# Keeping the second softmax map's exponentials in PSUM, and a third buffer for turned probabilities

## The chip, the cores and the metric

The kernel runs on one core of one Trainium2 chip. The core has a matrix engine (TensorE, in the profile PE, with PEld for its weight loads), a vector engine (DVE), an activation engine (ACT), a general engine (POOL) and a queue that issues DMA transfers (SP). SBUF is the working memory; PSUM is the memory that matmuls write, of which this kernel uses eight banks. The metric is the time of one execution on the device in microseconds (us); the time given is the median of several runs.

## The reference

Two layers over 512 latent tokens and 256 context tokens of width 1024, all in 32 bits. Layer 0 mixes tokens by differential attention, layer 1 by grouped-query attention with normed queries and keys. The change touches layer 0:

```python
def diff(qq, kk, vv, gate):
    o1 = sweep_attention(qq[..., 0, :], kk[..., 0, :], vv)
    o2 = sweep_attention(qq[..., 1, :], kk[..., 1, :], vv)
    o = o1 - lam.astype(o1.dtype) * o2
    o = rms_norm(o, subln_g) * (1.0 - lam_init)
    o = o.reshape(o.shape[0], o.shape[1], BRANCH_WIDTH)
    return (o * jax.nn.silu(gate)) @ w_out

y = diff(q, k_all, v_all, z)
yc = diff(qc, kc, vc, zc) if with_ctx_out else None
```

Each of the 8 heads has two maps of queries and keys, 64 wide, and one value of width 128. `sweep_attention` is softmax attention. Latent queries read 768 keys (latent and context), context queries read the 256 context keys. Around the mixer stand an adaptive norm before, projections of width 4096 into queries, keys, values and gate, an output projection, a norm after, and the gated residual.

## The kernel before

**The work in layer 0.** A head's attention is cut into units of 128 queries: four units (`s_units`, `unit(qt)`) for the latent queries, of which the last two (`CTX_AT`) carry 128 context queries along in heads 0 to 6. In head 7 the context queries have two small units of their own (`unit_last`). One unit does this, for the two maps m = 0 and 1:

- PE writes the scores of both maps into two PSUM tiles `sc[0]` and `sc[1]` of two banks each (`s_mm`, twelve matmuls, 18 with context queries). There are only these two tiles, so the next unit writes the same ones. The first matmul of a block writes `sc[1]`. Four more banks (`bk`) serve all other matmuls.
- DVE takes the maximum of each row, ACT the exponential with that maximum as bias and the row's sum as second output. For m = 0 it goes to one half of the pair tile `pp`, for m = 1 to a tile `p` (tag `p1`, two buffers). For context queries m = 0 goes to a tile of tag `p0`, m = 1 into the tile `ct` (tag `at128`), which later takes the turned probabilities.
- DVE inverts the sums and, for m = 1, multiplies by minus lambda (`nlam`). POOL scales the first map (`scaled(EP0, ...)`). Then one DVE operation combines them: pp = p * factor + pp. This is called the combination here.
- After two units `turn` transposes the pair tile in blocks on DVE, stores it to DRAM (`dr<-pp`) and loads it back in four transfers (`at<-dr`), so that keys lie on partitions. `at` has `ATB` = 2 buffers of 6144 bytes a partition; the two `p1` buffers have 3072 each.
- `pv_steps` splits `at` into a rounded part `ah` and a rest `al` (ACT and DVE), which PE multiplies with the values, three matmuls for a product.

Every product in the kernel is such a sum of three matmuls of rounded parts. PE also does the projections of queries, keys, values and gate for later heads in the same stretch; their weights come by DMA as `raw` and are split into `whi` and `wlo` by ACT and POOL or DVE. Tiles of tag `tmp`, three buffers, serve the swapped queries, the gate's silu, the squares of the head norm and others.

**What sets the order.** The program lists every operation first (`Plan`), with a duration for each by kind and size and the operations that it must wait for: those whose data it needs and those that still use its buffer. PSUM counts by bank: operations of different engines on one bank follow each other. `flow` lists the steps of the streams (scores, turned tiles, value products, others) by due times, with the projections between them. `plan` then simulates all engines, each taking the ready operation of the smallest key. The keys come from the best of twelve passes; then each number in `MOVES` seeds one random shift of some keys (`shift`), on PE or on DVE, ACT, POOL or SP. The resulting order is fixed in the program for each engine and for SP. The program's waits are made from the same list.

In the profile nearly all instructions have line L519, that of the helper which issues them, so the groups are told apart by tile names.

Of the kernel before, what the change touches and what calls it, by code (L numbers as in the profile page):

```python
# [9 lines left out]
F32 = mybir.dt.float32  # L10
F32R = mybir.dt.float32r
AF = mybir.ActivationFunctionType
# [4 lines left out]
P = 128  # L17
# [3 lines left out]
C = 256  # L21
T = 768
# [63 lines left out]
ATB = 2  # L86
# [8 lines left out]
def f32(ap):  # L95
# [37 lines left out]
SLACK = 0  # L133


# [470 lines left out]
def tile_backbone(  # L606
# [25 lines left out]
    def nm(s):  # L632
        uid[0] += 1
        return f"{s}_{uid[0]}"
# [7 lines left out]
    def small(n=1, tag="sm"):  # L642
        return sm.tile([P, 8], F32, tag=tag, name=nm("sm"), bufs=dict(sm=8, ss=6, l=6, mx=6, nmx=4)[tag])[:, :n]
# [19 lines left out]
    def sc2():  # L663
        scs.append(scs.pop(0))
        return scs[-1]
# [21 lines left out]
                d, b = o, a[:, e * 256:e * 256 + 256]  # L687
            nc.tensor.matmul(d, v[:, kt + e, c], b, start=first and i == 0, stop=last and i == 5)

    def turn(pool, pp, w=384, at=None):  # L690
        flat = pp.rearrange("p b u x -> p (b u x)")
        nc.vector.transpose(flat, flat)
        if at is None:
            at = pool.tile([P, 4, w], F32, tag=f"at{w}", name=nm("at"), bufs=ATB if w == 384 else 1)
        for lo in range(0, 4, 4 // DRSPLIT):
            n = 4 // DRSPLIT
            dr = drp.tile([P // DRSPLIT, 4 * 384], F32, tag="dr", name=nm("dr"), bufs=DRB)[:, :4 * w]
            nc.sync.dma_start(dr, flat[32 * lo:32 * (lo + n), :])
            for a in range(4):
                nc.sync.dma_start(  # L700
                    at[32 * a:32 * a + 32, lo:lo + n, :],
                    dr.rearrange("(q j) (a c) -> a j q c", j=32, c=w)[a])
        return at
# [9 lines left out]
    def unit_view(pp, u):  # L713
        return pp[:, :, u, :]
# [542 lines left out]
    for pr in range(NQT):  # L1257
        kts = (2 * pr, 2 * pr + 1)
        if pr + 1 < NQT:
            cs = nxt  # L1260
# [39 lines left out]
    with pl.pool("t0") as t0:  # L1300
# [147 lines left out]
        def s_mm(sc, h, qt, lo, w, prev):  # L1448
            qh, ql, kh_, kl_ = qk[h]
            tok = slice(qt * P, (qt + 1) * P)  # L1450
            for i, (a, b) in enumerate(((qh, kh_), (qh, kl_), (ql, kh_))):
                for m in (1, 0):
                    r = slice(m * 64, m * 64 + 64)
                    o = flat_sc(sc[m])[:, lo:lo + w]
                    if qt < NQ:
                        b_ = b[r, lo:lo + w]
                    else:
                        o, b_ = by_a(o, 64), by_a(b[r, :], 192)[:, :, P:]
                    with after(prev), chained(prev):
                        prev = nc.tensor.matmul(o, a[r, tok], b_, start=i == 0, stop=i == 2)  # L1460
            return prev

        def flat_sc(t):
            return t.rearrange("p j n -> p (j n)")
# [3 lines left out]
        def s_units(h, qts):  # L1468
            res, pair = [], {}
            if qts[0] == 0:  # L1470
                ctx_at[h] = []

            def unit(qt):
                e = CTX_AT.get(qt) if h < KT - 1 else None
                l = small(4, "l")
                sc = [sc2(), sc2()]
                prev = s_mm(sc, h, qt, 0, 512, None)
                prev = s_mm(sc, h, qt, 512, C, prev)
                if e is not None:
                    s_mm(sc, h, NQ + e, T, C, prev)  # L1480
                if (h, qt) in GRP_AT:
                    grp_mm(GRP_AT[h, qt])
                if e is not None:
                    if e == 0:
                        ctx_tiles[h] = (
                            t0.tile([P, 8, 2, 32], F32, tag="p0", name=nm("pp"), bufs=1),
                            t0.tile([P, 4, P], F32, tag="at128", name=nm("at"), bufs=1))
                    cp_, ct = ctx_tiles[h]
                    cs = [unit_view(cp_, e), ct.rearrange("p a c -> p (a c)")[:, e * C:e * C + C].rearrange("p (b x) -> p b x", x=32)]
                if qt % 2 == 0:  # L1490
                    pair[0] = t0.tile([P, 24, 2, 32], F32, tag="pp", name=nm("pp"), bufs=PPB)
                ps_ = [unit_view(pair[0], qt % 2), t0.tile([P, T], F32, tag="p1", name=nm("p"), bufs=2).rearrange("p (b x) -> p b x", x=32)]
                n = 1 if e is None else 2
                for m in range(2):
                    mx = small(2, "mx")
                    for j in range(n):
                        src = flat_sc(sc[m])[:, j * T:j * C + T]
                        nc.vector.tensor_reduce(mx[:, j:j + 1], src, AX.X, ALU.max, negate=True)
                        nc.scalar.activation(
                            (cs if j else ps_)[m], src.rearrange("p (b x) -> p b x", x=32), AF.Exp, bias=mx[:, j:j + 1],  # L1500
                            accum_out=l[:, 2 * m + j:2 * m + j + 1])
                    r = l[:, 2 * m:2 * m + n]
                    nc.vector.reciprocal(r, r)
                    if m == 1:
                        nc.vector.tensor_scalar(r, r, nlam, None, ALU.mult)
                    for j in range(n):
                        d, a = (cs if j else ps_)[0], (cs if j else ps_)[1]
                        if m == 0:
                            scaled(EP0, d, d, r[:, j:j + 1])
                        else:  # L1510
                            nc.vector.scalar_tensor_tensor(d, a, r[:, j:j + 1], d, ALU.mult, ALU.add)
                if qt % 2:
                    res.append(turn(t0, pair[0]))
                if e == 1:
                    ctx_at[h].append(turn(t0, cp_, P, ct))

            def unit_last(qt):
                if qt == NQ:
                    sts["sc"] = sc2()
                    pair[2] = t0.tile([P, 2, C], F32, tag="p0", name=nm("p"), bufs=1)  # L1520
                l = small(2, "l")
                qh, ql, kh_, kl_ = qk[h]
                tok, prev, ps_ = slice(qt * P, (qt + 1) * P), None, []
                sc = sts["sc"]
                for i, (a, b) in enumerate(((qh, kh_), (qh, kl_), (ql, kh_))):
                    for m in (1, 0):
                        r = slice(m * 64, m * 64 + 64)
                        with after(prev), chained(prev):
                            prev = nc.tensor.matmul(k_a_j(sc[:, m, :C]), a[r, tok], by_k(b[r, :], 2), start=i == 0, stop=i == 2)
                for m in range(2):  # L1530
                    mx = small(1, "mx")
                    nc.vector.tensor_reduce(mx, sc[:, m, :C], AX.X, ALU.max, negate=True)
                    if m == 0:
                        pt = pair[2][:, qt - NQ]
                    else:
                        pt = t0.tile([P, T], F32, tag="p1", name=nm("p"), bufs=2)[:, :C]
                    nc.scalar.activation(pt, sc[:, m, :C], AF.Exp, bias=mx, accum_out=l[:, m:m + 1])
                    ps_.append(pt)
                    r = l[:, m:m + 1]
                    nc.vector.reciprocal(r, r)  # L1540
                    if m == 0:
                        scaled(EP0, pt, pt, r)
                    else:
                        nc.vector.tensor_scalar(r, r, nlam, None, ALU.mult)
                        nc.vector.scalar_tensor_tensor(ps_[0], pt, r, ps_[0], ALU.mult, ALU.add)
                res.append(ps_[0])

            if qts[0] == NQ:
                if h < KT - 1:
                    return ctx_at[h], []  # L1550
                sts = {}
                return res, [Step(lambda qt=qt: unit_last(qt), 0.5) for qt in qts]
            return res, [Step(lambda qt=qt: unit(qt), 1.2 + 0.4 * (h < KT - 1 and qt in CTX_AT) + 1.0 * ((h, qt) in GRP_AT)) for qt in qts]

        def pv_steps(h, at, ch, after, ts, ms):
# [164 lines left out]
        for h in range(KT):  # L1720
            per = ATT + DL0[h] + sum(7.7 if f[0] == 'z' else 15.4 for f in HF0[h] if f != ('qk', 1))
            span = per - GAP0
            for ch in range(3):
                at, u = s_units(h, (2 * ch, 2 * ch + 1))
# [97 lines left out]
    for qi, (c, n) in enumerate(OUTC[:2]):  # L1822
        w = get_wout(0, c, n) if qi else w_o
# [18 lines left out]
    c, n = OUTC[2]  # L1842
    w = get_wout(0, c, n)
# [73 lines left out]
    with pl.pool("t1", "right") as t1p:  # L1917
# [281 lines left out]
        for h in range(KT):  # L2199
            p, j = h // 2, h % 2  # L2200
# [3 lines left out]
            for ch in range(2):  # L2204
                at, u = s1_units(h, (2 * ch, 2 * ch + 1))
# [21 lines left out]
        for qi, (c, n) in enumerate(OUTC1):  # L2227
            w = get_wout(1, c, n) if qi else w_o
# [3 lines left out]
            for m in range(NQ):  # L2232
# [13 lines left out]
                if qi == 2:  # L2246
# [6 lines left out]
                    for j in (1, 0):  # L2253
                        for h in range(2 if m == NQ - 1 else 1):
                            w_ = 256 if m == NQ - 1 else 512
                            a = h * w_
# [124 lines left out]
```

## Time and profile before

| | |
|---|---|
| median of 3 runs | 743.32 us (740.20, 743.32, 744.13) |
| the profiled execution's own time | 740.91 us |
| its span, from the first to the last instruction | 739.1 us |
| granted TensorE clock | 0.998 |
| DMA | 133.85 MB, 181 GB/s in the mean |

The profile shows one execution. "Busy" is the time in which an engine had an instruction running. Matmuls are pipelined and their ends modelled, so that a busy PE need not be at its peak. Rows of the timeline give start, duration, engine, line, operation, tile written <- tiles read, shapes and count, and in brackets the idle time before with what ended it. Rows of waits give who waited for whom: us in total, times, longest.

### The profile page before, as it was taken

To read this page: it belongs to the slowest core of one execution; us is meant where nothing else is said; L and a number is where in the kernel's file an instruction comes from. 1 tells how busy PE (TensorE), PEld (TensorE's weight loads), DVE (VectorE), ACT (ScalarE), POOL (GpSimd) and SP (SyncE) were. 2 spreads that over 40 slices of the span, in tenths; PEclk is the share of its full clock that TensorE was granted. 3 is DMA by queue.
4 is the path that set the end of the run, shared out by engine and by line. 5 is a ranking of instruction groups with operands and counts; after the bars stand their busy time and mean duration, and the time that the engine had idled before them with its cause. 6 is when DMAs were issued, how large, how long until landed. Compare 5 with 4: busy or idle time off the path is not lost. (4 is left out here: it accounts for less than half of the span.)

```text
span 739.1 us, 13953 instructions
## 1 busy us (share of the span) xinstructions
PE 726.0 (98%) x5030; PEld 651.1 (88%) x5030; DVE 551.7 (75%) x882; ACT 478.4 (65%) x1085; POOL 461.8 (62%) x506
## 2 busy tenths in 40 slices
PE   7999999999999999999999999999999999999996
PEld 6789888889888889888988998899999989898986
DVE  5454897969979796688887843689666789988834
ACT  6635557876678564676749853695366678788641
POOL 4454887788598856669753311466889969665201
PEclk9999999999999999999999999999999999999999
DMA  9932446255648387473757162453437678888503
GB/s 352 407 134 100 143 132 212 96 162 184 230 142 250 127 246 216 131 228 136 228 150 229 50 236 86 144 179 115 143 129 231 175 237 244 230 259 255 154 29 114
DMA packets 52884, 133.85 MB, mean 181 GB/s; under 512 B 6608, under 2 KB 28368, under 8 KB 51280
## 3 DMA queue, kind: packets, MB, share of 16 engines
q1 hardware_dynamic: 49248, 127.82, 54.1%
q10 hardware_dynamic: 3568, 5.16, 2.2%
q8 instruction: 39, 0.64, 0.4%
q14 instruction: 29, 0.24, 0.1%
HBM read 98.61 MB, written 30.15 MB: 174 GB/s over the span
## 5 line engine op out<-in xcount | busy, mean ns | idle before, releaser
L519 PE MATMUL bk<-whi,h 128*128 128x256 f32 (+1 forms) x1184 | 244.9, 298 | 2.6 <-ACT h L519 1.3
L519 PE MATMUL bk<-h,whi 128*128 128x512 f32 (+2 forms) x832 | 222.6, 348 | 0.0
L519 POOL TENSOR_TENSOR wlo<-raw,whi 128x256 fp32r<-128x256 f32 x200 | 169.2, 869 | 53.1 <-ACT whi L519 52.2
L519 PEld LDWEIGHTS bk<-whi,h 128*128 128x128 f32 x1184 | 191.0, 189 | 11.9 <-ACT h L519 2.1
L519 PE MATMUL bk<-wlo,h 128*128 128x256 f32 (+1 forms) x592 | 174.7, 298 | 0.0
L519 PEld LDWEIGHTS bk<-h,whi 128*128 128x128 f32 x832 | 144.7, 188 | 14.9 <-issue 1.7
L519 PE MATMUL bk<-h,wlo 128*128 128x512 f32 (+2 forms) x416 | 144.1, 348 | 0.0
L519 DVE TENSOR_REDUCE sm<-sc 128x1 f32<-128x768 f32 (+1 forms) x128 | 101.9, 813 | 21.0 <-PE sc L519 14.1
L519 PEld LDWEIGHTS bk<-wlo,h 128*128 128x128 f32 x592 | 111.1, 188 | 4.0
L519 DVE TENSOR_TENSOR al<-at,ah 128x512 fp32r<-128x512 f32 x103 | 96.2, 952 | 19.2 <-ACT ah L519 11.6
L519 POOL TENSOR_SCALAR pp<-pp,sm 128x768 f32<-128x768 f32 (+1 forms) x78 | 77.5, 996 | 52.6 <-DVE sm L519 29.7
L519 PEld LDWEIGHTS bk<-h,wlo 128*128 128x128 f32 x416 | 78.3, 188 | 7.0
L519 ACT CAST whi<-raw 128x1024 fp32r<-128x1024 f32 (+1 forms) x70 | 71.7, 1025 | 17.5 <-PE bk L519 7.8
L519 ACT CAST ah<-at 128x512 fp32r<-128x512 f32 x103 | 61.6, 621 | 9.8 <-PE bk L519 5.7
L519 DVE STREAM_TRANSPOSE pp<-pp 128x1536 f32<-128x1536 f32 (+1 forms) x39 | 61.4, 1575 | 3.8 <-POOL pp L519 3.7
L519 POOL TENSOR_TENSOR sz<-sz,za 128x384 f32<-128x384 f32 (+1 forms) x24 | 30.4, 1265 | 38.3 <-ACT za L519 31.6
L519 PEld LDWEIGHTS sc<-qk,qk 64*128 64x128 f32 x480 | 37.3, 185 | 15.8 <-ACT p L519 3.2
L519 ACT ACTIVATE jk<-bk 128x128 f32<-128x128 f32 (+4 forms) x66 | 22.7, 345 | 43.9 <-PE bk L519 25.6
L519 PE MATMUL sc<-qk,qk 64*128 64x256 f32 (+1 forms) x480 | 48.4, 338 | 1.1 <-ACT p L519 1.0
L519 ACT ACTIVATE pp<-sc,sm 128x768 f32<-128x768 f32 (+1 forms) x46 | 35.5, 772 | 20.2 <-DVE sm L519 20.1
L519 DVE SCALAR_TENSOR_TENSOR pp<-p,sm,pp 128x768 f32<-128x768 f32 x32 | 43.6, 1363 | 3.2 <-POOL pp L519 2.4
L519 ACT ACTIVATE za<-za 128x384 f32<-128x384 f32 (+1 forms) x72 | 39.8, 560 | 5.2 <-DVE za L519 4.9
(213 smaller groups left out, 1353.2 us busy)
## 6 DMA issues: line engine op xcount, KB each, us to landing
dr<-pp SPq DMA_DIRECT2D x32, 768.0 KB, 4.2
at<-dr SPq DMA_DIRECT2D x128, 192.0 KB, 4.6
raw<-in_a_w SPq DMA_DIRECT2D x30, 512.0 KB, 4.4
araw<-in_ada_g SPq DMA_DIRECT2D x12, 1024.0 KB, 6.2
raw<-in_b_w SPq DMA_DIRECT2D x20, 512.0 KB, 3.7
ag<-in_ada_s SPq DMA_DIRECT2D x16, 512.0 KB, 9.5
raw<-in_w_out SPq DMA_DIRECT2D x16, 512.0 KB, 3.8
sw<-qr ACTq DMA_DIRECT2D x32, 128.0 KB, 3.1
```

What stands on the lines that cost most here:

```text
L519: self.ops.append(getattr(eng, meth)(*args, **kw))
```

## The change

- In `unit`, the second map's exponentials (m = 1) are written over their own scores in `sc[1]`, for latent and for context queries. The combination reads them there: one input from PSUM, one from SBUF. So `sc[1]` is in use until the combination has ended, where it was in use until the exponential had. `ct` is written by its transfers alone.
- The tile of tag `p1` is gone. `unit_last`, which used it too, takes a tile of tag `tmp`.
- `turn` has a parameter for the number of buffers of `at`. Layer 0 passes 3, which takes the bytes that `p1` had; layer 1 keeps 2.
- `MOVES` is longer: its 308 numbers are kept, and 207 are added behind them. No operation is added or taken away, and the list of operations is in the same order; the order within each engine comes out anew from the plan.

```diff
-    855299187, 174445339, 702593093, 709254020, 236711175, 391571874)
+    855299187, 174445339, 702593093, 709254020, 236711175, 391571874, 802471119, 806597346, 795014970, 909414891,
...
+    426925270, 219226640, 492092606)

-    def turn(pool, pp, w=384, at=None):
+    def turn(pool, pp, w=384, at=None, n=ATB):
...
-            at = pool.tile([P, 4, w], F32, tag=f"at{w}", name=nm("at"), bufs=ATB if w == 384 else 1)
+            at = pool.tile([P, 4, w], F32, tag=f"at{w}", name=nm("at"), bufs=n if w == 384 else 1)
...
-                    cs = [unit_view(cp_, e), ct.rearrange("p a c -> p (a c)")[:, e * C:e * C + C].rearrange("p (b x) -> p b x", x=32)]
+                    cs = unit_view(cp_, e)
...
-                ps_ = [unit_view(pair[0], qt % 2), t0.tile([P, T], F32, tag="p1", name=nm("p"), bufs=2).rearrange("p (b x) -> p b x", x=32)]
+                ps_ = unit_view(pair[0], qt % 2)
...
+                        src = src.rearrange("p (b x) -> p b x", x=32)
                         nc.scalar.activation(
-                            (cs if j else ps_)[m], src.rearrange("p (b x) -> p b x", x=32), AF.Exp, bias=mx[:, j:j + 1],
+                            src if m else cs if j else ps_, src, AF.Exp, bias=mx[:, j:j + 1],
                             accum_out=l[:, 2 * m + j:2 * m + j + 1])
...
-                        d, a = (cs if j else ps_)[0], (cs if j else ps_)[1]
+                        d = cs if j else ps_
                         if m == 0:
                             scaled(EP0, d, d, r[:, j:j + 1])
                         else:
+                            a = flat_sc(sc[m])[:, j * T:j * C + T].rearrange("p (b x) -> p b x", x=32)
                             nc.vector.scalar_tensor_tensor(d, a, r[:, j:j + 1], d, ALU.mult, ALU.add)
                 if qt % 2:
-                    res.append(turn(t0, pair[0]))
+                    res.append(turn(t0, pair[0], n=3))
...
-                        pt = t0.tile([P, T], F32, tag="p1", name=nm("p"), bufs=2)[:, :C]
+                        pt = t0.tile([P, 512], F32, tag="tmp", name=nm("p"), bufs=3)[:, :C]
```

20 rows, old and new, of the table MOVES are left out of this document.

## The prediction, made before any run of the changed kernel

> **What bounds the kernel now.** I read the page's busy times first, then busy time by stretch (65 to 408 us holds the first layer's attention, 408 to 700 us its output and most of the second layer), then the waits of the weight loads in the same two stretches.
>
> ```profile
> PE 726.0 (98%) x5030; PEld 651.1 (88%) x5030; DVE 551.7 (75%) x882; ACT 478.4 (65%) x1085; POOL 461.8 (62%) x506
> 65.00:408.00 343.00, 341.88 (x2396) 299.76 (x2396) 282.90 (x419) 227.73 (x491) 248.41 (x229) 1.00 0.57 177
> 408.00:700.00 292.00, 290.38 (x1992) 272.38 (x1991) 221.93 (x361) 204.23 (x503) 178.31 (x217) 1.00 0.58 180
> ```
>
> After each stretch's length come the busy times of PE, PEld, DVE, ACT and POOL. In the stretch that the change touches PE stands still for 343.00 - 341.88 = 1.12 us, in the next for 292.00 - 290.38 = 1.62 us. DVE is busy for 82% of the first stretch, POOL for 72%, and both stay behind PE. So PE's own work bounds the kernel. What an edit off PE can win is the wait in front of PE. Of the waits before weight loads (us, times, longest) these are the two of score blocks for exponentials from 65 to 408 us, and the four longest after 408 us:
>
> ```profile
> PEld sc L519 <- ACT p L519: 3.2, 7, 0.8
> ...
> PEld sc L519 <- ACT at L519: 1.2, 2, 0.8
> ```
>
> ```profile
> PEld bk L519 <- ACT sz L519: 1.2, 2, 1.0
> PEld bk L519 <- ACT ah L519: 0.7, 2, 0.4
> PEld bk L519 <- DVE kn L519: 0.6, 1, 0.6
> PEld sc L519 <- ACT pp L519: 0.6, 2, 0.4
> ```
>
> Nine score blocks of layer 0 wait for the exponentials of the unit before: 3.2 + 1.2 = 4.4 us. The four rows of the rest come to 3.1 us. That is 7.5 us in all, my upper end for what better orders can take away, since a weight load partly waits under a matmul that still runs; the smaller measure is PE's own idle time, 1.12 + 1.62 = 2.74 us.
>
> **The change part by part.** One unit (one head, 128 queries) of layer 0, PE, DVE, ACT and POOL rows together, starts at 221.55 us:
>
> ```profile
> 221.55 1.32 PE L519 MATMUL sc<-qk,qk 64*128 64x512 f32 x12
> ...
> 223.27 1.80 DVE L519 TENSOR_REDUCE sm<-sc 128x1 f32<-128x768 f32 x2
> ...
> 224.24 0.90 ACT L519 ACTIVATE pp<-sc,sm 128x768 f32<-128x768 f32 x1
> ...
> 225.13 0.89 ACT L519 ACTIVATE p<-sc,sm 128x768 f32<-128x768 f32 x1
> ...
> 225.41 0.63 PE L519 MATMUL bk<-h,whi 128*128 128x512 f32 x2
> ...
> 225.64 0.19 PEld L519 LDWEIGHTS bk<-h,wlo 128*128 128x128 f32 x1
> 225.71 1.07 POOL L519 TENSOR_SCALAR pp<-pp,sm 128x768 f32<-128x768 f32 x1 [0.62 <-DVE sm L519]
> 225.87 0.39 PE L519 MATMUL bk<-h,wlo 128*128 128x512 f32 x1
> ...
> 226.42 1.31 PE L519 MATMUL sc<-qk,qk 64*128 64x512 f32 x12
> ...
> 226.81 1.02 DVE L519 SCALAR_TENSOR_TENSOR pp<-p,sm,pp 128x768 f32<-128x768 f32 x1 [0.25 <-POOL pp L519]
> ```
>
> The two bk rows of PE in between show its pace: two 512-wide matmuls begin within 225.87 - 225.41 = 0.46 us. Now the second map's exponentials go to SBUF (p), so the next unit's scores start at 226.42, 0.40 us after the exponential ends (225.13 + 0.89 = 226.02) and before the combining operation on DVE (pp from p, sm, pp) has begun.
>
> *The new wait.* With p in the scores' place, the next scores must wait for that operation: here until 226.81 + 1.02 = 227.83, 6.28 us after the unit's start where it was 4.87. This is the shortest chain a unit can have as the engines stand: two maxima, two exponentials, POOL's scaling of the first map, the combination. Behind a waiting score matmul stands every later one of PE's program, and whatever waits for their results; so the chain costs nothing only if other matmuls are put in front. Is there room? The last head is the tightest place (PE's four blocks and a later row, the DVE rows, POOL's, POOL's scaling as a group with busy us and mean ns after its first bar, and the score matmuls in the tile's view: min/median/max, first and last start):
>
> ```profile
> 368.48 1.32 PE L519 MATMUL sc<-qk,qk 64*128 64x512 f32 x12
> ...
> 373.11 1.31 PE L519 MATMUL sc<-qk,qk 64*128 64x512 f32 x12
> ...
> 379.24 1.33 PE L519 MATMUL sc<-qk,qk 64*128 64x512 f32 x12 [0.61 <-ACT p L519]
> ...
> 383.91 1.31 PE L519 MATMUL sc<-qk,qk 64*128 64x512 f32 x12
> ...
> 411.76 0.51 PE L519 MATMUL bk<-h,whi 128*128 128x384 f32 x2
> ```
>
> ```profile
> 373.72 2.68 DVE L519 SCALAR_TENSOR_TENSOR pp<-p,sm,pp 128x768 f32<-128x768 f32 x1
> ...
> 379.88 1.01 DVE L519 SCALAR_TENSOR_TENSOR pp<-p,sm,pp 128x768 f32<-128x768 f32 x1
> ...
> 386.34 1.01 DVE L519 SCALAR_TENSOR_TENSOR pp<-p,sm,pp 128x768 f32<-128x768 f32 x1
> ```
>
> ```profile
> 373.76 1.84 POOL L519 TENSOR_TENSOR gT<-gT,sz 128x768 f32<-128x768 f32 x1
> 378.60 0.91 POOL L519 TENSOR_SCALAR pp<-pp,sm 128x768 f32<-128x768 f32 x1 [3.00 <-DVE sm L519]
> ```
>
> ```profile
> L519 POOL TENSOR_SCALAR pp<-pp,sm 128x768 f32<-128x768 f32 x64 | 67.5, 1055 | 52.6 <-DVE sm L519 29.7 <-PE bk L519 5.4 <-ACT sz L519 3.6
> ```
>
> ```profile
> L519 PE MATMUL sc<-qk,qk x480: 270/280/502, 72.7 to 393.9; 64*128 64x256 f32 x96, 64*128 64x512 f32 x64
> ```
>
> The blocks stand 4.63, 6.13 and 4.67 us apart; at 6.4 us each (6.28 and a hand-over) the three move by 1.8, 0.3 and 1.7, 3.8 us together. Projection matmuls of the gate (bk from h, whi, 384 wide) still run at 411.76, 27 us after the last block, and need no score; they can go in front. Over all heads there is more room: from the first of the 480 score matmuls, 72.7, to head 7's at 368.48 are seven heads, 42.3 us each, and their four units take about 30: two of 6.4, and two with context queries of about 8.5, an estimate (four operations 256 wide more, some half a microsecond each). So I put the wait's exposed part at what the nine waiting blocks gain in scatter: POOL's scaling takes 1055 ns in the mean against 0.91 us at 378.60, 0.145 us more. 9 x 0.145 = 1.3 us. Ends: 0 (all covered) and 3.8 + 1.3 = 5.1 us (head 7 uncovered). Late next would be POOL's scaling, which now stands in PE's way and used to be free to wait.
>
> *The prices of the operations.* From the groups (busy us and mean ns after the first bar), and from the tile's view:
>
> ```profile
> L519 DVE TENSOR_REDUCE sm<-sc 128x1 f32<-128x768 f32 x96 | 88.8, 945 | 13.8 <-PE sc L519 13.2
> ...
> L519 DVE SCALAR_TENSOR_TENSOR pp<-p,sm,pp 128x768 f32<-128x768 f32 x32 | 43.6, 1363 | 3.2 <-POOL pp L519 2.4
> ...
> L519 ACT ACTIVATE p<-sc,sm 128x768 f32<-128x768 f32 x32 | 28.8, 900 | 2.8 <-DVE sm L519 2.8
> ...
> L519 DVE SCALAR_TENSOR_TENSOR pp<-at,sm,pp 128x256 f32<-128x256 f32 x14 | 9.7, 691 | 0.0
> ...
> L519 DVE TENSOR_TENSOR u<-bk,gate 128x512 f32<-128x512 f32 x10 | 6.9, 686 | 17.3 <-ACT jk L519 17.3
> ```
>
> ```profile
> L519 DVE SCALAR_TENSOR_TENSOR pp<-p,sm,pp x32: 1006/1077/2682, 78.1 to 391.9; 128x768 f32<-128x768 f32 x32
> ```
>
> The combination with both inputs in SBUF takes 1.01 us alone and 2.68 beside POOL's 1.84 us multiply. With one input in PSUM the nearest rows are u from bk and gate (512 wide, 686 ns) and the maximum from sc (768 wide, 945 ns); on their line 768 wide costs about 0.95 us and 256 wide 0.43. DVE is relieved of 32 x (1.36 - 0.95) + 14 x (0.69 - 0.43) = 13.1 + 3.6 = 17 us. None of it is on PE's path, so I count 0; ends 0 and what it lets the orders win, counted there. [...]
>
> The exponential into PSUM has no row: ACT never writes PSUM here. I take the 0.90 us of its SBUF form, the nearest; the upper end is 1.80, if one bank served its read and its write in turns; a little less than 0.90 is not excluded and would win nothing on PE. At 0.90 the sum is 0. [...]
>
> *The third buffer* (at, turned probabilities). Who waits for the present two? Of the tile's readers and of the DMA queue, 65 to 408 us:
>
> ```profile
>   DMA at<-dr: 1.4, 1
> ```
>
> ```profile
> SPq L519 <- DMA dr<-pp: 41.0, 14, 6.2
> ...
> SPq L519 <- DVE al L519: 0.9, 1, 0.9
> ```
>
> A reader waited for the transfer once, 1.4 us, and PE not at all. The loads of at wait for their own store (dr from pp, 41 us). Only one wait ended with the last reader, al: 0.9 us. So 0 for the time; the ends are -0.9 and 0. An earlier load issues no more DMAs, but their order with the weight loads on SP can change.
>
> *The last head's context units* put p (256 wide, two of them) among the three "tmp" buffers: 0, since gate work covers it; if that were gone, one combination, 0.5 us.
>
> *The orders.* Some 207 further shifts change priorities on all queues, in both layers. No row prices them. I take the smaller measure of PE's idle time away, -2.7 us, because only that is PE time; ends -7.5 and +2.7 (as much idle time again, since the old shifts were drawn for another graph of waits).
>
> Sum: +1.3 + 0 + 0 + 0 + 0 - 2.7 = -1.4 us. The profiled execution took 740.91 us (span 739.1), so 739.5; the median of the three runs, 743.32, lies 2.4 us above it, so I predict 743.3 - 1.4 = 741.9 us. Runs 740.2 to 744.1 us apart let no difference under about 0.5%, 3.7 us, be told from none.
>
> **The rivals.** *Slower: scores wait for the combination.* Place: the blocks of the last head and others as close. Price: 3.8 + 1.3 = 5.1 us with nothing won back, 748.4 us. For it: the present distances of 4.63 and 4.67 us are shorter than the chain. Against it: 27 us of gate work to put between. It decides once PE stands more than 3.7 us longer before scores.
>
> *Faster: all the waits go.* DVE's 17 us and the spare buffer let the orders take the 7.5 us of weight-load waits, at the chain's cost of 1.3: 743.3 - 6.2 = 737.1 us. For it: PEld is busy for only 299.76 of 343 us. Against: a 512-wide matmul holds PE for 0.23 us and its weight load takes 0.19, so weight loading idles where PE does not; PE is idle for 1.12 us. [...]
>
> *The exponential in place is slow* (1.80 us). Then the chain is 7.3 us, the three blocks of head 7 move by 2.7 + 1.2 + 2.6 = 6.5, and the time is 743.3 + 6.5 + 1.3 = 751.1 us. Nothing in the rows speaks for it but that none speaks against.
>
> **How the numbers follow.** Forecast (within 3.7 us of before) 0.53, faster rival 0.28, wait rival 0.15, slow exponential 0.04. So faster by over 0.5% 0.28, within 0.53, slower 0.19. The range takes in the faster rival, with the ends of third buffer and orders down to 743.3 - 7.5 - 0.9 = 734.9, and the wait rival up to 748.4. The forecast's own range is 739.6 to 747.0.
>
> **What would show it.** Combinations of about 0.95 us, none near 2.7; exponentials onto sc at 0.90; weight loads before scores that wait for DVE pp where they waited for ACT p, near 5.7 us in sum; score blocks in the last head 6.4 us apart or more; PE still idle for about 1 us in layer 0. I am wrong if PE's idle time in layer 0 grows by more than 3.7 us, or if the span shrinks where PE was already full.

## The result, and the profile after

Six runs of the changed kernel took 747.85 to 754.07 us, median 751.03; six of the kernel before on the same chip 740.20 to 744.13, median 742.27. The ratio is 1.0114, with a 95% interval of 1.0078 to 1.0149: slower by 1.1%, where no change within 0.5% (741.9 us) was predicted. On another chip (below) it was 746.90 to 740.60, ratio 1.0077 (1.0053 to 1.0101). The profiled execution took 751.58 us, its span is 749.8 where it was 739.1.

The page's busy times of the changed kernel, and then busy time by stretch (after each stretch's length PE, PEld, DVE, ACT, POOL, then granted clock, DMA share, GB/s):

```profile
PE 731.7 (98%) x5030; PEld 651.9 (87%) x5030; DVE 543.9 (73%) x882; ACT 479.8 (64%) x1085; POOL 446.7 (60%) x506
```

By stretch:

```profile
65.00:408.00 343.00, 336.40 (x2362) 294.31 (x2361) 258.83 (x393) 219.22 (x468) 225.86 (x227) 1.00 0.55 172
408.00:700.00 292.00, 291.29 (x1986) 270.84 (x1985) 224.61 (x371) 209.03 (x515) 183.92 (x220) 1.00 0.58 178
```

PE has the same 5030 matmuls and now stands still for 343.00 - 336.40 = 6.60 us in layer 0, where it was 1.12; in the next stretch for 0.71 where it was 1.62. So the idle time that came is made before 408 us. It is half of the profile's loss: of the 10.7 us by which the span grew, 5.0 are idle time of PE and 5.7 are PE's own busy time (726.0 to 731.7). The granted clock was 0.995 where it was 0.998, worth about 2 us by my estimate (749.8 x 0.005 - 739.1 x 0.002); the rest of the busy time was not traced.

DVE's relief came and bought nothing. Its combinations fell from 43.6 + 9.7 to 32.4 + 6.6 us, 14.3 us less, and its busy time over the whole execution by 7.8 us, since other operations of it took longer. (The 24 us by which the first stretch fell, 282.90 to 258.83, also hold work that moved out of the stretch.)

Who made PE wait from 65 to 408 us (us, times, longest), first in the kernel before, then in the changed one:

```profile
PE sc L519 <- ACT p L519: 1.0, 2, 0.6
```

```profile
PE bk L540 <- ACT sz L540: 3.8, 3, 3.2
PE sc L540 <- DVE pp L540: 2.0, 3, 0.9
PE bk L540 <- ACT arow L540: 0.5, 1, 0.5
PE bk L540 <- DVE al L540: 0.2, 1, 0.2
```

And the weight loads of score blocks, for the combination, where the prediction looked for 5.7 us:

```profile
PEld sc L540 <- DVE pp L540: 3.7, 6, 1.2
```

The second row of PE's is the wait that the change adds. The first holds one wait of 3.22 us, which can be followed back through three engines. Rows of the timeline of DVE, POOL, ACT and PE, in that order:

```profile
220.39 5.27 DVE L540 TENSOR_TENSOR al<-at,ah 128x512 fp32r<-128x512 f32 x1
225.58 2.36 DVE L540 STREAM_TRANSPOSE pp<-pp 128x1536 f32<-128x1536 f32 x2
...
228.76 0.54 DVE L540 SCALAR_TENSOR_TENSOR za<-sz,za 128x384 f32<-128x384 f32 x1
...
220.45 1.87 POOL L540 TENSOR_TENSOR qk<-qr,qk 128x768 fp32r<-128x768 f32 x1
222.26 2.85 POOL L540 TENSOR_TENSOR wlo<-raw,whi 128x256 fp32r<-128x256 f32 x4
...
229.34 0.52 ACT L540 ACTIVATE za<-za 128x384 f32<-128x384 f32 x1 [5.35 <-DVE za L540]
...
232.51 0.50 PE L540 MATMUL bk<-h,whi 128*128 128x256 f32 x2 [3.22 <-ACT sz L540]
```

A subtraction that takes 692 ns in the median lasts 5.27 us. It ends 0.55 us after the last of five POOL instructions that run back to back beside it. I call that a hold: an operation that lasts far longer than its like while another engine works. DVE's next operations come late, ACT stands before `za` and with it its copy `sz` of a PSUM bank, which frees the bank that PE needs.

The operations' prices (min/median/max in ns) are as forecast, combination and exponential in place:

```profile
L540 DVE SCALAR_TENSOR_TENSOR pp<-sc,sm,pp x46: 443/1007/1020, 72.4 to 405.5; 128x768 f32<-128x768 f32 x32, 128x256 f32<-128x256 f32 x14
...
L540 ACT ACTIVATE sc<-sc,sm x46: 434/865/888, 70.4 to 402.4; 128x768 f32<-128x768 f32 x32, 128x256 f32<-128x256 f32 x14
```

### The profile page after: what moved, and what is told of

It reads as the page before. It is cut to its first block, busy times and chain, and to the rows that moved or that the text cites. A ratio compares the mean times of both kernels' runs of the same rounds, so it can differ in the third digit from the quotient of the medians.

```text
span 749.8 us, 13948 instructions
## 1 busy us (share of the span) xinstructions
PE 731.7 (98%) x5030; PEld 651.9 (87%) x5030; DVE 543.9 (73%) x882; ACT 479.8 (64%) x1085; POOL 446.7 (60%) x506
## 4 chain that ended last, share of the span: by engine, by line
PE 48%; ACT 1%; DVE 1%; issue 1%; DMA 1%; DVEq 0%; ACTq 0%
PE bk L540 39%; PE sc L540 9%; DMA araw<-in_ada_g 1%; DVE pp L540 0%; DVE sm L540 0%; DVE al L540 0%; ACT jk L540 0%; ACT pp L540 0%; ACT za L540 0%; DVE u L540 0%; ACT sm L540 0%; ACT ah L540 0%; ACT whi L540 0%; ACT qk L540 0%; ACT sz L540 0%
## 5 line engine op out<-in xcount | busy, mean ns | idle before, releaser
L540 PE MATMUL bk<-h,whi 128*128 128x512 f32 (+2 forms) x832 | 226.1, 350 | 4.0 <-ACT sz L540 3.4
L540 POOL TENSOR_TENSOR wlo<-raw,whi 128x256 fp32r<-128x256 f32 x200 | 164.6, 848 | 41.6 <-ACT whi L540 36.0
L540 POOL TENSOR_SCALAR pp<-pp,sm 128x768 f32<-128x768 f32 (+1 forms) x78 | 74.9, 965 | 60.9 <-DVE sm L540 58.8
L540 DVE TENSOR_TENSOR al<-at,ah 128x512 fp32r<-128x512 f32 x103 | 97.7, 967 | 13.2 <-ACT ah L540 10.7
L540 POOL TENSOR_TENSOR sz<-sz,za 128x384 f32<-128x384 f32 (+1 forms) x24 | 28.1, 1171 | 44.0 <-ACT za L540 42.5
L540 DVE SCALAR_TENSOR_TENSOR pp<-sc,sm,pp 128x768 f32<-128x768 f32 (+1 forms) x46 | 38.2, 847 | 4.5 <-POOL pp L540 2.8
```

Source lines behind the costliest of these rows:

```text
L540: self.ops.append(getattr(eng, meth)(*args, **kw))
```

## The experiments

Theory O: the loss lies in the new orders. Theory W: it lies in the scores' longer hold, whatever the order. Theories C, N and S came up on the way. Every kernel ran in five rounds beside the kernel before, on several chips; ratios are to the kernel before on the same chip. The code shown is shortened: where an edit changes an operation, the order is still planned with the operation as it was, and only what is issued in that order changes.

### The orders as they stand: the long hold and the start

The first edit moves one operation of DVE (number 2191, the `al` above) behind `za` (2102); the second takes before's order up to 32 us on PE and 40 us elsewhere; the third does both.

```diff
-        em.chain(pl.plan())
+        order = pl.plan()
+        at = {o.n: o for o in order}
+        order.remove(at[2191])
+        order.insert(order.index(at[2102]) + 1, at[2191])
+        em.chain(order)
```

> The changed kernel as it is, for a second profile on another day of the chip. Theory O (the new orders make the loss): the long hold of the combination of halves (al from at, ah) at 220 us, 5.3 us, PE's 3.2 us of idle time at 232 us and the half clock behind it stand in this profile too, because the order of every engine is fixed; time about 751 us, 1.011 of before. Theory C (chance: the hold and the half clock are accidents of one execution): the profile shows neither, and the time still is 751. Theory W (the scores' wait for the combining operation makes the loss): says nothing on this run but that weight loads wait for DVE pp for about 3.7 us again.

> One operation of VectorE is moved in the changed kernel's order: the al that was held for 5.27 us at 220.39 us comes four operations later, behind the two transposes, gT and za. Theory O: al takes about 0.7 us, za on VectorE comes about 5 us earlier, ScalarE no longer waits 5.35 us for it, PE's idle 3.2 us at 232 us goes, and with it the half clock (about 1.5 us of slow matmuls): 751.0 - 4.7 = 746.3 us, 0.994 of the changed kernel. Theory W: PE next waits for something else at the same place, as the scores are late anyway; 750 to 751 us. Theory C: no change of the time, 751 us.

> The changed kernel with the order of before on every queue for the first part (up to 32 us on PE, 40 us on VectorE, ScalarE and POOL, 40 us on SP's queue), and its own order from there on. Theory O: the half clock at 18.6 to 22 us and PE's two waits at the start go, 2.2 us less: 748.8 us, 0.997 of the changed kernel. Theory W: the start holds no scores, and the loss stays: 751 us. Theory C (the phase of the clock at the start differs from execution to execution): 751 us, and half clock at the start in some profiles whatever the order.

> Both edits together: the one operation al moved behind za, and the order of before up to about 40 us. Theory O: the two gains add, 751.0 - 4.7 - 2.2 = 744.1 us, 0.991 of the changed kernel and level with before within 0.3%. Theory W: 750 to 751 us. Theory C: 751 us.

Measured: after_again 746.90 us, al_later 747.25 (1.0079, 1.0059 to 1.0099), old_start 746.56 (1.0076, 1.0053 to 1.0099), both edits 746.52 (1.0072, 1.0047 to 1.0097). None differs from the changed kernel on this chip (after_again); al_later comes near theory O's 746.3 us only because that was counted from the first chip's 751.0. The hold stands in the second profile too, with the same 5.27 and 3.22 us, and the move takes it away, `al` and PE's row in al_later:

```profile
226.70 1.23 DVE L541 TENSOR_TENSOR al<-at,ah 128x512 fp32r<-128x512 f32 x1
...
231.12 0.50 PE L541 MATMUL bk<-h,whi 128*128 128x256 f32 x2 [0.48 <-ACT sz L541]
```

PE stands still for 3.5 us in layer 0 instead of 6.2 (339.52 and 336.76 busy of 343), and the median does not move. In old_start, where that part of the order is as in the changed kernel, the same `al` took 2.00 us, ending 0.55 us after the first of POOL's five, and PE waited 0.66. So the hold depends on how the engines happen to meet: 5.27 us in two profiles, 2.00 us in this one. The profiled execution of after_again (750.30 us) was the slowest of its six, the others took 745.46 to 747.40. The largest wait on the page was not what sets the median. Whether the unprofiled executions had it isn't shown.

### Undoing a part in a fixed order, and both kernels without shifts

p_sbuf and two_at keep the changed kernel's order on every queue. Both issue the loads of `at` into two buffers; p_sbuf also writes the second map's exponentials to SBUF (one buffer for 768 wide, two for 256). x_before0 and x_after0 have an empty `MOVES`.

```diff
-                    res.append(turn(t0, pair[0], n=3))
+                    res.append(turn(t0, pair[0], n=2))
...
-                            src if m else cs if j else ps_, src, AF.Exp, bias=mx[:, j:j + 1],
+                            p1[j] if m else cs if j else ps_, src, AF.Exp, bias=mx[:, j:j + 1],
```

> The order of every queue is the changed kernel's, but the second map's exponentials go to SBUF again (the room for it is taken from the third buffer, so turned probabilities have two). So a score block is free as soon as the second exponential has ended, about 1.1 us or more before the combination has. Theory W (the loss is PE's wait for the combination): those waits go and most of the loss with them; 1.001 to 1.003 of before. Theory O (the loss lies in the orders: many short waits for split weights, h, al and sz, which do not come from the scores): the score waits go (3.7 us in the weight loads' view, about 1 us of PE), the combination is back at 1.0 to 2.7 us, and the time stays within 1.5 us of the changed kernel, 1.006 to 1.010 of before.

> The order of every queue is the changed kernel's, the exponentials stay in PSUM, and turned probabilities have two buffers in place of three. Theory O with the third buffer worth nothing by itself: 1.006 to 1.010 of before, as the changed kernel. If the new orders lean on the third buffer (loads of at issued earlier than the last reader), SP's queue waits for DVE al at several places and PE waits for halves of at: 2 us or more slower than the changed kernel, 1.011 or above. Theory W: as the changed kernel.

> Before with the planner's order alone, without any of the later shifts. To be read against x_after0. Theory O: the shifts are worth several us in either kernel, so this one takes 746 to 752 us.

> The change with the planner's order alone, without any of the shifts: so the two kernels differ in exponentials in PSUM and a third buffer, planned in the same way. Theory W (the longer hold of the scores costs): slower than x_before0 by 4 us or more. Theory O (only the shifts differ in quality): level with x_before0 within 2 us, on either side.

Measured: p_sbuf 762.48 us (1.0277, 1.0247 to 1.0307), two_at 754.77 (1.0175, 1.0146 to 1.0204). In the changed order each part of the change gains: PSUM 762.48 - 754.77 = 7.7 us (with one buffer for the exponentials where before has two), the third buffer 1.0175 against 1.0077, about 7 us (4.5 against the first chip's 1.0114). With two buffers SP's queue and PE wait where they did not. SP's row of the changed kernel from 65 to 408 us, the same row of two_at, and PE's first rows of two_at over the whole execution:

```profile
SPq L540 <- DVE al L540: 1.2, 1, 1.2
```

```profile
SPq L541 <- DVE al L541: 23.0, 3, 12.8
```

```profile
PE bk L541 <- ACT qr L541: 2.9, 1, 2.9
PE bk L541 <- ACT gT L541: 2.1, 2, 1.6
```

And the combination with both inputs in SBUF meets POOL again, up to 2.5 us in p_sbuf (the one of 2.51 us starts at 378.56 us, beside a POOL `qk` of 1.85 us from 378.40 on):

```profile
L541 DVE SCALAR_TENSOR_TENSOR pp<-p,sm,pp x46: 467/1132/2507, 71.9 to 412.7; 128x768 f32<-128x768 f32 x32, 128x256 f32<-128x256 f32 x14
```

So the order was made for the change and leans on it, which theory W did not foresee. But x_before0 took 753.52 us (1.0161, 1.0130 to 1.0192) and x_after0 760.37 (1.0258, 1.0224 to 1.0292): with the same planner and no shifts at all the change is 6.9 us slower, which theory O did not foresee. Still, PE's busy time differs by 0.7 us in layer 0 (339.25 and 338.52 of 343) and by 2.0 us from 408 to 700 us (286.92 and 284.95 of 292), where the code is the same: two orders differ by chance as well, fixed stretches hold somewhat different work, and the pair alone settles nothing.

### Orders searched in the same way for both

> Before's code with 131 further shifts of the order, kept one by one when the planner priced the order cheaper on average over its nominal prices and four draws in which some VectorE operations are held and transfers late. Theory O (the 6 us between the two kernels are the luck of two orders, not the price of the edits): orders searched in the same way bring both kernels to the same time within 2 us; this one 736 to 742 us. Theory W (holding the scores until the combination costs time whatever the order): this one is 4 us or more below re_after.

> The changed kernel's code with 160 further shifts, searched in the same way with as many tries. Theory O: most of the ten short waits of PE (0.3 to 0.9 us each) go, and it comes down from 746.9 to 738 to 742 us, within 2 us of re_before. Theory W: the waits of scores for the combination stay and others take the place of those that went; 743 us or more, 4 us or more above re_before.

> A second search for before's code from another start of the draw, 125 further shifts. It shows how far two orders of the same kernel, searched alike, lie apart. Theory O: 1 to 3 us from re_before on either side, as much as the difference between the kernels. Theory W: within 1 us of re_before, and below both re_after.

> A second search for the changed code, 133 further shifts. Theory O: 1 to 3 us from re_after, 739 to 743 us, no clear distance from the two re_before. Theory W: 743 us or more.

Measured: re_before 740.96 us (1.0003, 0.9989 to 1.0018), re_before2 742.34 (1.0013, 0.9989 to 1.0037); re_after 745.57 (1.0062, 1.0045 to 1.0078), re_after2 746.67 (1.0080, 1.0064 to 1.0097). Two orders of one kernel lie 1.1 to 1.4 us apart, the kernels 3.2 to 5.7. Theory O falls, as far as two orders of each can show it: with orders searched alike the change still costs 4 to 5 us. (Both searches started from the shifts at hand, and of the changed kernel's 515 the first 308 had been drawn for before; but without any shifts the change cost 6.9 us.) And further shifts won nothing for before's own code: both its intervals hold 1. Layer 0 of re_before and re_after, and what made PE wait in re_after and in re_after2:

```profile
65.00:408.00 343.00, 343.00 (x2406) 301.48 (x2405) 279.87 (x420) 228.68 (x491) 249.15 (x230) 1.00 0.56 178
```

```profile
65.00:408.00 343.00, 339.23 (x2393) 297.26 (x2392) 257.91 (x403) 226.05 (x480) 227.59 (x230) 1.00 0.54 177
```

```profile
PE sc L556 <- DVE pp L556: 2.2, 3, 1.1
PE bk L556 <- DVE al L556: 1.1, 1, 1.1
PE bk L556 <- ACT sz L556: 0.4, 1, 0.4
```

```profile
PE sc L553 <- DVE pp L553: 2.2, 3, 0.9
```

What the search could not remove is the wait for the combination, and two such waits stand at the same places in all three orders of the changed code (its own, re_after's, re_after2's): near 141 us and between 370 and 378 us. Theory W seemed right. But why there? At 140.83 us in the changed kernel, rows of DVE, POOL and PE:

```profile
137.84 1.33 DVE L540 TENSOR_SCALAR sm<-sm,nlam 128x2 f32<-128x2 f32 x1
139.28 1.41 DVE L540 SCALAR_TENSOR_TENSOR pp<-sc,sm,pp 128x768 f32<-128x768 f32 x2
...
137.26 1.88 POOL L540 TENSOR_TENSOR qk<-qr,qk 128x768 fp32r<-128x768 f32 x1
...
140.83 1.32 PE L540 MATMUL sc<-qk,qk 64*128 64x512 f32 x12 [0.79 <-DVE pp L540]
```

And at 377.52 us:

```profile
372.37 1.79 DVE L540 TENSOR_SCALAR sm<-sm,nlam 128x2 f32<-128x2 f32 x1
374.26 1.02 DVE L540 SCALAR_TENSOR_TENSOR pp<-sc,sm,pp 128x768 f32<-128x768 f32 x1
375.32 1.78 DVE L540 STREAM_TRANSPOSE pp<-pp 128x1536 f32<-128x1536 f32 x1
377.02 0.44 DVE L540 SCALAR_TENSOR_TENSOR pp<-sc,sm,pp 128x256 f32<-128x256 f32 x1
...
372.28 1.86 POOL L540 TENSOR_TENSOR qk<-qr,qk 128x768 fp32r<-128x768 f32 x1
...
377.52 1.32 PE L540 MATMUL sc<-qk,qk 64*128 64x512 f32 x12 [0.90 <-DVE pp L540]
```

At both places the combination does not wait for POOL's scaling, as the prediction had it, but for a multiply of two numbers a partition, 1/sum times `nlam`, that ends when POOL's `qk` ends. (At the second place a transpose of 1.78 us also stands between the two combinations. The third waits are smaller; re_after2's, 0.60 us at 231.87 us, does follow POOL's scaling.) The multiply's groups in the kernel before and in the changed kernel, busy us and mean ns after the bar:

```profile
L519 DVE TENSOR_SCALAR sm<-sm,nlam 128x2 f32<-128x2 f32 x14 | 6.9, 493 | 0.3
```

```profile
L540 DVE TENSOR_SCALAR sm<-sm,nlam 128x2 f32<-128x2 f32 x14 | 9.7, 691 | 0.5
L540 DVE TENSOR_SCALAR sm<-sm,nlam 128x1 f32<-128x1 f32 x20 | 4.2, 211 | 0.5
```

Only the form of two columns is long; it belongs to the units with context queries. Before has it too, but no score waited for it there, since the exponential had freed `sc[1]`. The reciprocal of the same two columns, just before it, never took over 0.17 us.

### The small multiply

Theory N: these waits are the multiply's. const_re_after gives it a constant (-0.2, so that the second map's weight is not the reference's), lam_re_after takes it off DVE, start_re_after and lam_start_re_after put re_before's order in front, up to 85 us.

```diff
-                        nc.vector.tensor_scalar(r, r, nlam, None, ALU.mult)
+                        nc.vector.tensor_scalar(r, r, -LAM_INIT, None, ALU.mult)     # const_re_after
...
-            (nc.vector if eng == "v" else nc.gpsimd).tensor_scalar(dst, src, s_, 1.0, ALU.mult, ALU.mult)
+            (nc.vector if eng == "v" else nc.gpsimd).tensor_scalar(dst, src, s_, ninv, ALU.mult, ALU.mult)     # lam_re_after
...
-                    nc.scalar.copy(*heads_out(gT[h][:, sl], o, moved))
+                    nc.scalar.activation(*heads_out(gT[h][:, sl], o, moved), AF.Copy, scale=nlam)     # lam_re_after
```

> The order of re_after, with one operand changed: the small multiply of the second map's reciprocals (sm from sm and nlam, 128 x 1 or 2) takes a constant, -0.2, in place of the computed nlam; so the weight of the second map is not the reference's. Theory N (PE's waits for the combination come from this small multiply, which reads two tiles of SBUF and is held behind POOL's 1.85 us qk: 1.40 us at 138.0 and 1.82 us at 365.3 where 0.2 is usual): the multiply takes 0.2 us everywhere, PE's waits of 0.86 us at 141 and 1.11 us at 370.5 go, 745.6 - 2.0 = 743.6 us, 0.997 of re_after. Theory W (the chain of a unit is too long for PE whatever the multiply takes): the two waits stay within 0.3 us of what they were; 745 to 746 us.

> The order of re_after, with the multiply by nlam taken off VectorE: POOL's scaling of the first map multiplies by 1/nlam as well, and ScalarE's copy of the attention's output (gT from bk) by nlam. Theory N: as const_re_after or up to 0.7 us better, since the small operation goes altogether, unless POOL's scaling with a second scalar from SBUF takes longer than 1.06 us; 742.9 to 743.8 us. Theory W: 745 to 746 us.

> The code of the change in the order of re_after, but with re_before's order on every queue up to 85 us (projections of the start, first head). Theory S (a part of the loss is the start, which the change does not touch: PE's gaps before 20 us sum to 6.7 us in the changed kernels and to 5.2 us in re_before): 745.6 - 1.5 = 744.1 us. Without it (the start differs from execution to execution): 745.6 us within 0.5.

> lam_re_after and start_re_after together. Theories N and S both: 745.6 - 2.0 - 1.5 = 742.1 us, 1.0 to 1.5 us above re_before, the rest being single waits for al and sz. Theory W with S: 744 us. Neither: 745.6 us.

Measured: const_re_after 746.00 us (1.0058, 1.0035 to 1.0082). The constant did nothing, PE's waits for the combination came to 2.8 us, and the reason given for the hold, two tiles read from SBUF, falls: with one tile and a constant the form of two columns is as long, that of one column (26, six of them not this multiply) not.

```profile
L559 DVE TENSOR_SCALAR sm<-sm 128x2 f32<-128x2 f32 x14 | 8.9, 635 | 0.3
...
L559 DVE TENSOR_SCALAR sm<-sm 128x1 f32<-128x1 f32 x26 | 3.9, 149 | 6.0 <-ACT junk L559 5.4
```

Why the form of two columns is held (635 ns in the mean) and that of one is not (149) no run shows. The multiply has these two widths alone in the runs.

lam_re_after took 744.76 us (1.0044, 1.0027 to 1.0062). The waits went, from 2.2 us to the row below, but the time fell by 0.8 us only, which its interval does not tell from nothing. PE's wait of 1.1 us for `al` stayed (1.3), and other engines pay: the copy with a factor takes 474 ns where the plain one takes 372, 24 times, and POOL's scaling 983 where it took 912 (medians).

```profile
PE sc L559 <- DVE pp L559: 0.3, 1, 0.3
```

start_re_after took 757.16 us (1.0209, 1.0180 to 1.0237) and lam_start_re_after 755.36 (1.0193, 1.0161 to 1.0226), 13 us over what theory S expected. Three score blocks wait for the combination at the end of re_before's part:

```profile
78.86 1.31 PE L592 MATMUL sc<-qk,qk 64*128 64x512 f32 x12 [1.81 <-DVE pp L592]
...
86.94 1.67 PE L592 MATMUL sc<-qk,qk 64*128 64x512 f32 x18 [1.26 <-DVE pp L592]
...
94.75 1.65 PE L592 MATMUL sc<-qk,qk 64*128 64x512 f32 x6 [5.13 <-DVE pp L592]
```

The first two stand where re_before has its blocks 4.59 and 6.76 us apart, as before's buffers allow, and wait 1.81 + 1.26 = 3.1 us. The third, 5.13 us, stands at the seam of the two orders: about 1 us of other matmuls is left in front of it, where re_before has 8.41 us between the blocks. So the runs are a miss as a test of the start; the first two waits price the new wait where PE's order is not made anew.

### The multiply in two halves, and before's order at the start

```diff
-                        nc.vector.tensor_scalar(r, r, nlam, None, ALU.mult)
+                        for j in range(r.shape[1]):
+                            nc.vector.tensor_scalar(r[:, j:j + 1], r[:, j:j + 1], nlam, None, ALU.mult)
```

> The order and the arithmetic of re_after; only the multiply by nlam on two columns (128 x 2, 651 ns in the mean, 14 times) is issued as two on one column each (the 128 x 1 form takes 210 ns in the mean, 20 times). Theory N (that a VectorE multiply of even width is held by a POOL instruction and one of a single column is not, and that this hold sets PE's waits for the combination): no multiply over 0.25 us, PE's waits of 0.86 us at 141 us and 1.11 us at 370.5 us go, 745.6 - 2.0 = 743.6 us at best; as lam_re_after, which took away the same waits and came to 744.8 us, 743.6 to 744.8 us. Theory W (the chain is too long anyway): waits within 0.3 us of what they were, 745 to 746 us.

> split_re_after with before's order on every queue for the first 24 us of PE alone (no score block is among them). Theory S (the start of the changed orders costs: PE waits 0.55 us for row, 0.59 us for h and 0.65 us more for xt than in re_before, and the TensorE clock is at half for 3.4 us from 18 us on in the profiles of the changed orders): those waits are as in before, no half clock at 18 us, 1.5 to 2 us less than split_re_after, 742 us. If the half clock comes from chance: as split_re_after within 0.5 us.

Measured: split_re_after 744.10 us (1.0030, 1.0013 to 1.0046), where re_after has 1.0062 (1.0045 to 1.0078): about 1.5 to 2.4 us less, by the medians and by the ratios, with intervals that just touch. The group of the multiply, its place beside POOL's `qk` near 137 us, layer 0, and all that made PE wait in it:

```profile
L559 DVE TENSOR_SCALAR sm<-sm,nlam 128x1 f32<-128x1 f32 x48 | 8.8, 208 | 0.9
```

```profile
136.78 0.34 DVE L559 TENSOR_SCALAR sm<-sm,nlam 128x1 f32<-128x1 f32 x2
...
136.30 1.86 POOL L559 TENSOR_TENSOR qk<-qr,qk 128x768 fp32r<-128x768 f32 x1
```

```profile
65.00:408.00 343.00, 342.49 (x2419) 300.71 (x2420) 255.22 (x423) 229.17 (x488) 231.81 (x231) 1.00 0.57 178
```

```profile
PE bk L559 <- ACT sz L559: 0.4, 1, 0.4
```

PE waits for no combination any more and stands still for 0.5 us in layer 0, less than the 1.12 us of before. This profiled execution took 741.48 us, less than the median; that of split_start_re_after took 745.42 us, more than its median of 742.19, and shows 0.4 us of such waits and 1.24 us of idle time. The transpose between the two combinations is still there and PE does not wait. So theory N is shown for the waits: one operation more in a unit, and the two waits that no order had removed are gone (its "even width" is shown for two columns alone). That these waits are worth about 2 us of the median is less sure, as the intervals say.

split_start_re_after took 742.19 us (1.0020, 1.0000 to 1.0040), the 742 us of theory S, but not by its reasons. The granted clock from 18 to 22 us was 0.50 in its profile and 1.00 in split_re_after's, with the changed start, while before's own profile has 1.00 there and the changed kernel's 0.58: the half clock did not go with either start. The waits of 0.5 us for row and 0.6 us for h went, as expected, but one of 1.3 us for h came, as before has it, and PE's idle time before 65 us fell by 0.4 us only, from 4.0 to 3.7. Its 1.9 us below split_re_after lie within the two intervals, so that the start carries a part is not shown.

No version beat the kernel before; the best of the changed code is level with it within its interval.

## Why the prediction was wrong

**The orders, -2.7 us: the step that failed.** It took PE's idle time as what new orders win. They won nothing: before's own code with 131 and 125 further shifts took 1.0003 and 1.0013 of before's time. The changed kernel's order brought 5.5 us more idle time in layer 0 in its profile, 3.2 of them the one wait behind the held `al`; two further searches left 343.00 - 339.23 = 3.8 and, in re_after2, 2.7 us of idle time. The term's other end, +2.7 for orders drawn for another graph of waits, had the sign. That PE was at 1.12 us of idle time was the warning: there was nothing to win and a tuned order to lose.

**The new wait, +1.3 us: right in kind, too small, and for another reason.** PE waited 2.0 us for the combination in the changed kernel and 2.2 in both searched orders. The forecast spread the exposure over nine blocks by the scatter of POOL's scaling; it stood at three blocks, and at the two large ones behind the held multiply, which the prediction's chain of a unit left out. The chain of 6.28 us itself agrees with the trace: score blocks of the last head start at 377.52, 383.84 and 390.25 us, 6.32 and 6.41 apart. And that "the chain costs nothing only if other matmuls are put in front" held: in re_before's order over the first head, made without that wait, two blocks cost 3.1 us.

With 0 for the orders and about 2 us for the wait the prediction's sum gives +2 us, where orders searched alike measured 4 to 5. No term of the sum holds the rest.

**Prices: right.** Combination 1.007 us in the median (0.95 taken), the longest 1.020, none near 2.7; with both inputs in SBUF the longest was 2.682 in the kernel before. That one input in PSUM would do this was the author's estimate from rows of other operations; in the changed kernel's order p_sbuf, with both inputs in SBUF, has up to 2.507. Exponential in place 0.865 (0.90 taken), the longest 0.888. The slow-exponential rival is dead; that its 751.1 us is nearly the measured 751.03 is luck. In the changed kernel the exponential of 768 columns took 873 ns in the mean into PSUM and 904 into SBUF, 32 of each.

**DVE's 17 us, counted at 0: right.** The combinations took 14.3 us less and PE gained nothing. In re_before, where the old combinations are back, PE is busy for all 343.00 us of layer 0 in the profile.

**The third buffer, 0: wrong as a general price.** In before's order nothing waited for it. In the changed order it carries about 7 us, as two_at shows. Whether it gains anything over before by itself no run shows, as none was searched for two buffers.

**The rivals.** Slower by the scores' wait was the right side at the wrong size: 748.4 us by 5.1 us of waits, against 2.0 us of such waits in the changed kernel; the rest is PE's waits for `sz`, `arow` and `al` and its longer busy time. What would make the prediction wrong was named (PE's idle time in layer 0 up by more than 3.7 us), and it happened, 5.5, though only with the 3.2 us of the held `al`, whose going left the median unchanged.

What stays open: of the 4 to 5 us that the change costs in orders searched alike, the multiply accounts for about 2. The rest, 3.2 us at split_re_after and 1.3 at split_start_re_after, was not taken apart. A lower clock does not explain it: the granted clock was 0.997 in the mean of split_re_after's executions and of before's beside them.

## What to carry to other kernels

When a buffer's release moves from one operation to a later one, everything on the way to the later one joins the critical chain, the smallest operations too: look at each one's longest time in the profile, not at its usual one. Where PE was idle for 1 us of 343, relief of another engine was worth nothing here and a rewritten order was a risk; compare the two codes under orders searched alike before crediting either. And a wait that is the longest on the page can be one execution's: move it away and time it before believing it.

## What the runs showed of the hardware that was not expected

- A VectorE multiply of 128 x 2 numbers took up to 1.79 us behind a POOL instruction of 1.86, 691 ns in the mean over 14 with a tile as factor, 635 in another run with a constant; on one column it took 208 ns, 48 times, none over 0.22. A reciprocal of two columns never took over 0.17.
- A VectorE subtraction with two SBUF inputs was held for 5.27 us through five POOL instructions in a row, in two profiles at the same place; with a slightly different meeting it came through after the first of them, in 2.00 us (old_start, two_at).
- After 3.22 us of PE's idle time the granted clock was 0.66 from 233 to 238 us in the first profile of the changed kernel (a score block at 234.23 us took 2.29 us instead of 1.31), and 1.00 in the second, after the same idle time at the same place.
